# The first k tile for eight column groups, the second for two: another start of a fused decoder layer

## The chip, the cores and the metric

The kernel runs on one core of one Trainium2 chip. The time is device microseconds of one execution; the number given is the median of three runs. The profile shows one execution, whose own time stands beside it. Engines are named as in the profile: PE (TensorE, matmuls), PEld (its weight loads), DVE (VectorE), ACT (ScalarE), POOL, and SP, whose queue issues nearly all DMAs.

## The reference

One decoder layer on 256 tokens with a width of 2048, in float32. What matters here is its beginning:

```python
mod = silu(c) @ w_ada + b_ada            # (6*2048): shift1, scale1, gate1, shift2, scale2, gate2
h   = rms_norm(x, g1) * (1 + scale1) + shift1
p   = h @ w_in                           # 2048 x 12288, columns split into q, k, v, gates of two mixers
# retention and HGRN2 on p, gated, projected, merged, added to x
# then RMSNorm, modulation, w_up, causal conv of width 3, silu(a) * b, w_down, final RMSNorm
```

So the columns of scale1 and shift1 for 128 channels (a k tile) are needed before these channels of h can enter the product with w_in.

## The kernel before

**Tiles.** h has 16 k tiles of 128 channels. The stage around the change multiplies h with the 6144 columns of w_in that the two mixers need, as 12 groups of 512 columns (`ATT`): groups 0 and 1 are the forget gates of HGRN2, 2 and 3 its q, 4 and 5 its inputs, 6 to 11 q, k and v of retention. A piece is one k tile of one group (256 KB of weights). Groups 4, 5, 10 and 11 come out with tokens on the partitions (`mm_rows`, six matmuls of 512 columns for a piece: L187, L188, L189), the others with channels there (`mm_cols`, twelve matmuls of 256 columns: L200, L201, L202). Each product is made of three: high x high, high x low, low x high parts. ACT copies the loaded weights (`raw`) into their high part `wh` (L165), DVE subtracts to get the rest `wl` (L170). L200, L201, L187 and L189 need `wh` only, L202 and L188 need `wl`. There are 12 buffers of `raw`, 4 of `wh` and 4 of `wl`, each for up to two pieces.

**Modulation.** For each k tile, DVE makes four dots of silu(c) with rows of w_ada (L389, 1024 or 1025 columns and 512 KB each; `ada1` loads). ACT turns them into the scale (L400, L401) and the shift (L403) of that tile, and makes the high part of `hT` (L336) and the full value `h` (L340); DVE makes the low part (L341). DVE has multiplied x with the token's norm before (`times`, L379).

**Accumulators.** Groups 0 and 1 are RESIDENT: they stay in four PSUM tiles (`po`) over all 16 k tiles. All other groups share two PSUM tiles of 1024 columns (`pg`): a visit multiplies some k tiles, then `take` moves the sum to SBUF, the first time by an ACT copy (L700, `p<-pg`), later by a DVE addition (L702).

**Order.** The loop at L747 visits the groups in turn. `have` says up to which k tile a visit at the count `work` goes: one k tile more for each ADA_EVERY = 11 pieces. Ahead of the loop stands a part of its own (L705 to L744): the first FIRST = 4 groups take k tiles 0 and 1, both in PSUM, and then groups 2 and 3 are taken. Instructions that pass through `pin` while `self.ordered` is set keep the order in which they are written on their engine; the others (matmuls and `take` among them) are put in place by the scheduler when the program is built. On the chip each engine then runs its list from first to last.

After this stage come the gates' columns, the rest of the mixers, w_out, w_up and w_down.

Of the kernel before, what the change touches and what calls it, by code (L numbers as in the profile page):

```python
# [16 lines left out]
AF = mybir.ActivationFunctionType  # L17
# [12 lines left out]
G = 512  # L30
NORM_EPS = 1e-6
HEAD_EPS = 1e-5
FIRST = 4
RESIDENT = 2
ADA_EVERY = 11
LAG = 1
NOSYNC = mybir.DependencyInfo(mybir.DependencyClass.NoSync, mybir.DependencyReason.DATA)
SMALL = 70

# [16 lines left out]
class Kernel:  # L56
# [609 lines left out]
    def run(self):  # L666
        nc, a = self.nc, self.a
# [11 lines left out]
        def act(k):  # L679
            return hT[k // 2][:, k % 2, :]  # L680

        def ada1(k):
            if k > 0 and k % 2 == 0:
                ins = self.times(k, 2, rx_sb)
                self.tc.add_manual_dep(ins.ins, self.last.ins.name, NOSYNC, reason="behind the weights traced ahead of it")
            yield from self.scale_shift("ada1", k, s1, t1, self.gn1)
            if k % 2 == 0:
                hT[k // 2] = self.blk([P, 2, 2 * T], F32R, name="hT")
            self.modulated(act(k), self.xT[k // 4][:, k % 4, :], k, s1, t1)
            yield 0.7  # L690

        accs = [self.blk([P, NT, G] if c0 in ROWS else [P, 4, T], name="p") for c0 in ATT]
        done = [0] * len(ATT)
        mms = [self.mm_rows if c0 in ROWS else self.mm_cols for c0 in ATT]

        def take(g, ps, fresh):
            for at, z in self.parts(ps, ATT[g] in ROWS):
                dst = accs[g][:, at, :]
                if fresh:
                    nc.scalar.activation(dst, z, AF.Copy)  # L700
                else:
                    nc.vector.tensor_tensor(dst, dst, z, ALU.add)  # L702


        ada = [ada1(k) for k in range(KT)]  # L705
        for _ in range(3):
            next(ada[0])
        rx = self.token_rstd(parts)
        rx_sb = c.tile([P, T], F32, name="rx_sb")
        ps = [self.po2(), self.po2(), self.pg(), self.pg()][:FIRST]  # L710
        for k in range(2):
            for i in range(4 if k else 1):
                if k and i == 1:
                    self.times(k, 1, rx)
                next(ada[k])
            if k == 0:
                self.times(k, 1, rx)

            ahead = 2 * k
            uppers = [self.upper(a["wa"][g][:, k : k + 1, :], 1, G) for g in range(ahead + 1)]  # L720
            rests = [self.rest(z) for z in uppers[:ahead]]
            for _ in ada[k]:
                pass
            for g in range(FIRST):
                if g >= ahead:
                    rests.append(self.rest(uppers[g] if g < len(uppers) else self.upper(a["wa"][g][:, k : k + 1, :], 1, G)))
                wh, wl = rests[g]
                if k == g == 0:
                    self.pin(nc.scalar.activation(rx_sb, rx, AF.Copy))
                mms[g](ps[g], act(k), wh[:, 0, :], wl[:, 0, :], k == 0, k == 1 and g >= RESIDENT)  # L730
        for _ in range(2):
            next(ada[2])
        self.ordered = False
        for gen in ada[2:]:
            self.start(gen, 1)
        for g in range(FIRST):
            done[g] = 2
            if g >= RESIDENT:
                take(g, ps[g], True)
        self.pace(1, 4, ADA_EVERY / 2)  # L740
        self.pace(0, 3.5, 24)

        work = 2 * FIRST
        g = FIRST  # L744
        att, gates = [], []
        small = False
        while min(done) < KT:  # L747
            if work > SMALL and not small:
# [3 lines left out]
                self.start(self.lower_bound())  # L752
            have = min(KT, 2 + int((work - LAG) / ADA_EVERY))
            m = have - done[g]
# [18 lines left out]
            g = (g + 1) % len(ATT)  # L773
            if have == KT and done[0] < KT:
                g = min(i for i in range(len(ATT)) if done[i] < KT)
# [9 lines left out]
        for j in range(4):  # L785
            ps = self.rows(a["wb"][j], act)
# [55 lines left out]
        for j in range(4):  # L842
            last = j == 3
            x1.append(self.load_rows(j))
            g = self.row(self.gate["gate1"], j, "g1")
            ps = self.products(self.mm_rows, self.po2() if last else self.pg(), a["wout"][j], actm, 0, KT, hold=4 * last)
# [14 lines left out]
            if j == 2:  # L861
                part = self.row_part(ss)
# [232 lines left out]
```

## Time and profile before

| | |
|---|---|
| median of 3 runs | 1531.68 us (1531.55 to 1531.72) |
| profiled execution, its own time | 1532.02 us |
| its span | 1529.9 us |
| PE busy | 1511.9 us, 99% |
| DVE busy | 1178.0 us, 77% |
| ACT busy | 841.5 us, 55% |
| DMA | 385.68 MB, mean 252 GB/s |
| granted clock of PE | 0.998 |

The page's first part gives busy time by engine, its fourth the chain of work that ended last, followed back from the end. In a row of a group or of the timeline stand line, engine, operation, output and inputs, shapes and count; behind them, in groups, busy time and mean ns, then idle time ahead of them and what ended it; in the timeline, start and duration in us stand ahead, and a bracket gives the idle time ahead and what ended it. A start-to-start distance is often shorter than the duration, since the next instruction on an engine begins while the last one drains.

### The profile page before, as it was taken

What the parts mean: (1) busy time and instruction counts of PE and PEld (TensorE: products, weight loads), DVE (VectorE), ACT (ScalarE), POOL (GpSimd) and SP (SyncE); (2) the same over time, 40 slices, a digit from 0 to 9 for tenths busy, and PEclk for the clock granted to TensorE, in tenths of its full rate; (3) what the DMA queues carried; (4) which work ended last, traced back from release to release, by engine and by line L of the source; (5) the groups of instructions that cost most, each with busy time, mean ns of one, the idle gap of its engine ahead of it and who ended that gap; (6) DMA issues with size and microseconds to landing.
All of it is one profiled execution on the core that took longest, in us unless ns stands there. A gap on an engine that the chain in (4) does not pass through costs nothing.

```text
span 1529.9 us, 22149 instructions
## 1 busy us (share of the span) xinstructions
PE 1511.9 (99%) x8258; PEld 1304.4 (85%) x8258; DVE 1178.0 (77%) x1610; ACT 841.5 (55%) x1194; POOL 4.0 (0%) x8
## 2 busy tenths in 40 slices
PE   8999999999999999999999999999999999999997
PEld 6999999888888888888878888888888888888886
DVE  7899996997998977898767777777777769455454
ACT  6655455766865554445456565555556558344343
POOL 0000000000000000000000000000000000000000
PEclk9999999999999999999999999999999999999999
DMA  9999996777777789989947777777777766676651
GB/s 375 370 355 328 311 332 217 240 278 239 274 240 264 256 293 323 323 300 341 336 126 231 231 235 233 237 227 232 232 231 232 227 191 192 204 209 206 194 166 55
DMA packets 110992, 385.68 MB, mean 252 GB/s; under 512 B 12802, under 2 KB 13346, under 8 KB 110884
## 3 DMA queue, kind: packets, MB, share of 16 engines
q1 hardware_dynamic: 110016, 383.14, 76.1%
q8 instruction: 64, 1.05, 0.3%
q10 hardware_dynamic: 868, 1.13, 0.2%
q14 instruction: 44, 0.36, 0.1%
HBM read 382.11 MB, written 2.11 MB: 251 GB/s over the span
## 4 chain that ended last, share of the span: by engine, by line
PE 95%; ACT 2%; DVE 1%; DMA 1%; issue 0%; SPq 0%; DVEq 0%; ACTq 0%
PE pg L187 13%; PE pg L188 13%; PE pg L189 13%; PE po L935 11%; PE pg L935 10%; PE po L937 5%; PE pg L937 5%; PE po L189 3%; PE po L187 3%; PE po L188 3%; PE pg L202 3%; PE pg L200 3%; PE pg L201 3%; PE po L565 1%; PE po L200 1%; PE po L201 1%
## 5 line engine op out<-in xcount | busy, mean ns | idle before, releaser
L170 DVE TENSOR_TENSOR wl<-raw,wh 128x1024 fp32r<-128x1024 f32 (+1 forms) x536 | 635.2, 1190 | 286.6 <-ACT wh L165 282.4
L165 ACT ACTIVATE wh<-raw 128x1024 fp32r<-128x1024 f32 (+1 forms) x536 | 551.1, 1033 | 544.1 <-PE pg L189 189.0
L389 DVE SCALAR_TENSOR_TENSOR raw<-raw,sc 128x1024 f32<-128x1024 f32 x192 | 233.5, 1219 | 0.0
L935 PE MATMUL pg<-h2T,wh 128*128 128x512 f32 x704 | 221.6, 396 | 0.6 <-ACT h L371 0.6
L935 PE MATMUL po<-h2T,wh 128*128 128x512 f32 x704 | 221.1, 395 | 0.0
L187 PE MATMUL pg<-wh,hT 128*128 128x512 f32 x512 | 202.7, 396 | 0.2 <-ACT p L700 0.2
L188 PE MATMUL pg<-wl,hT 128*128 128x512 f32 x512 | 200.1, 391 | 0.7 <-DVE wl L170 0.7
L189 PE MATMUL pg<-wh,hT 128*128 128x512 f32 x512 | 199.8, 390 | 0.0
L937 PEld LDWEIGHTS pg<-h2T,wl 128*128 128x128 f32 x704 | 132.1, 188 | 31.7 <-DVE wl L170 0.5
L937 PEld LDWEIGHTS po<-h2T,wl 128*128 128x128 f32 x704 | 132.2, 188 | 31.3
L937 PE MATMUL pg<-h2T,wl 128*128 128x256 f32 x704 | 138.5, 278 | 0.1
L937 PE MATMUL po<-h2T,wl 128*128 128x256 f32 x704 | 138.3, 278 | 0.0
L188 PEld LDWEIGHTS pg<-wl,hT 128*128 128x128 f32 x512 | 96.3, 188 | 21.0 <-DVE wl L170 2.2
L189 PEld LDWEIGHTS pg<-wh,hT 128*128 128x128 f32 x512 | 96.1, 188 | 20.3
L187 PEld LDWEIGHTS pg<-wh,hT 128*128 128x128 f32 x512 | 96.2, 188 | 19.4 <-ACT p L700 0.4
L202 PE MATMUL pg<-hT,wl 128*128 128x256 f32 x384 | 109.1, 284 | 0.6 <-DVE wl L170 0.6
L200 PE MATMUL pg<-hT,wh 128*128 128x256 f32 x384 | 109.2, 284 | 0.1
L201 PE MATMUL pg<-hT,wh 128*128 128x256 f32 x384 | 109.0, 284 | 0.0
L935 PEld LDWEIGHTS pg<-h2T,wh 128*128 128x128 f32 x704 | 107.2, 189 | 0.8 <-ACT h L371 0.8
L935 PEld LDWEIGHTS po<-h2T,wh 128*128 128x128 f32 x704 | 107.2, 189 | 0.0
L202 PEld LDWEIGHTS pg<-hT,wl 128*128 128x128 f32 x384 | 74.1, 193 | 0.8 <-DVE wl L170 0.8
L200 PEld LDWEIGHTS pg<-hT,wh 128*128 128x128 f32 x384 | 74.2, 193 | 0.6 <-ACT wh L165 0.2
(229 smaller groups left out, 2192.0 us busy)
## 6 DMA issues: line engine op xcount, KB each, us to landing
raw<-in_wup SPq DMA_DIRECT2D x176, 512.0 KB, 4.5
raw<-in_wdown SPq DMA_DIRECT2D x88, 512.0 KB, 4.3
raw<-in_wa SPq DMA_DIRECT2D x80, 512.0 KB, 5.7
raw<-in_ada SPq DMA_DIRECT2D x64, 512.5 KB, 5.7
raw<-in_ada SPq DMA_DIRECT2D x64, 512.0 KB, 5.8
raw<-in_wab SPq DMA_DIRECT2D x64, 512.0 KB, 5.0
raw<-in_gate SPq DMA_DIRECT2D x32, 512.5 KB, 4.7
raw<-in_wb SPq DMA_DIRECT2D x32, 512.0 KB, 5.2
```

The lines of the kernel that those rows point to most:

```text
L165: self.pin(self.nc.scalar.activation(wh, raw, AF.Copy))
L170: self.last = self.nc.vector.tensor_tensor(wl, raw, wh.bitcast(F32), ALU.subtract)
L187: nc.tensor.matmul(ps[t], lhsT=hi, rhs=wh, start=first, stop=False)
L188: nc.tensor.matmul(ps[t], lhsT=hi, rhs=wl, start=False, stop=False)
L189: nc.tensor.matmul(ps[t], lhsT=lo, rhs=wh, start=False, stop=last)
L200: nc.tensor.matmul(out, lhsT=wh[:, cs], rhs=hi, start=opens, stop=False, skip_group_check=True)
L201: nc.tensor.matmul(out, lhsT=wh[:, cs], rhs=lo, start=False, stop=False, skip_group_check=True)
L202: nc.tensor.matmul(out, lhsT=wl[:, cs], rhs=hi, start=False, stop=last, skip_group_check=True)
L389: dot = self.pin(nc.vector.scalar_tensor_tensor(raw[:, 0, :], raw[:, 0, :], 1.0, self.sc[:, u * GW : u * GW + w], ALU.mult, ALU.mult, accu ...
L565: nc.tensor.matmul(ps[:, j * 64 : (j + 1) * 64], lhsT=(kt if n > 1 else k)[:, h, c * P : (c + 1) * P], rhs=eq[:, j * 64 : (j + 1) * 64], s ...
L935: self.pin(nc.tensor.matmul(ps[j + z], lhsT=wh[:, cs[z]], rhs=act, start=kt == 0, stop=False))
L937: nc.tensor.matmul(ps[j + z][:, :T], lhsT=wl[:, cs[z]], rhs=act[:, :T], start=False, stop=kt == KT - 1)
```

## The change

The first k tile now runs for eight groups, and the second only for groups 0 and 1, which stay in PSUM. FIRST becomes 8; groups 2 to 7 each get a `pg` tile, one k tile and a `take` at once. The dots of the second k tile are written between groups 3 to 6. `work` starts at 10 in place of 8 and LAG is 7 in place of 1, so the loop begins with group 8 and two k tiles, and the visits after it are of other sizes.

```diff
-FIRST = 4
+FIRST = 8
 RESIDENT = 2
 ADA_EVERY = 11
-LAG = 1
+LAG = 7
...
-        ps = [self.po2(), self.po2(), self.pg(), self.pg()][:FIRST]
-        for k in range(2):
-            for i in range(4 if k else 1):
-                if k and i == 1:
-                    self.times(k, 1, rx)
-                next(ada[k])
-            if k == 0:
-                self.times(k, 1, rx)
-
-            ahead = 2 * k
-            uppers = [self.upper(a["wa"][g][:, k : k + 1, :], 1, G) for g in range(ahead + 1)]
-            rests = [self.rest(z) for z in uppers[:ahead]]
-            for _ in ada[k]:
-                pass
-            for g in range(FIRST):
-                if g >= ahead:
-                    rests.append(self.rest(uppers[g] if g < len(uppers) else self.upper(a["wa"][g][:, k : k + 1, :], 1, G)))
-                wh, wl = rests[g]
-                if k == g == 0:
-                    self.pin(nc.scalar.activation(rx_sb, rx, AF.Copy))
-                mms[g](ps[g], act(k), wh[:, 0, :], wl[:, 0, :], k == 0, k == 1 and g >= RESIDENT)
+        ps = [self.po2(), self.po2()]
+
+        def one(g, k):
+            return self.upper(a["wa"][g][:, k : k + 1, :], 1, G)
+
+        next(ada[0])
+        self.times(0, 1, rx)
+        part = one(0, 0)
+        for _ in ada[0]:
+            pass
+        for g in range(FIRST):
+            wh, wl = self.rest(one(g, 0) if g else part)
+            if g == 0:
+                self.pin(nc.scalar.activation(rx_sb, rx, AF.Copy))
+            to = ps[g] if g < RESIDENT else self.pg()
+            mms[g](to, act(0), wh[:, 0, :], wl[:, 0, :], True, g >= RESIDENT)
+            if g >= RESIDENT:
+                take(g, to, True)
+            done[g] = 1
+            if g >= FIRST - 5 and g < FIRST - 1:
+                next(ada[1])
+            if g == FIRST - 5:
+                self.times(1, 1, rx)
+
+        rests = [self.rest(one(g, 1)) for g in range(RESIDENT)]
+        for _ in ada[1]:
+            pass
+        for g in range(RESIDENT):
+            wh, wl = rests[g]
+            mms[g](ps[g], act(1), wh[:, 0, :], wl[:, 0, :], False, False)
+            done[g] = 2
         for _ in range(2):
             next(ada[2])
         self.ordered = False
         for gen in ada[2:]:
             self.start(gen, 1)
-        for g in range(FIRST):
-            done[g] = 2
-            if g >= RESIDENT:
-                take(g, ps[g], True)
...
-        work = 2 * FIRST
+        work = FIRST + RESIDENT
```

How the built programs differ is seen on ACT first. Before, from the second group's `wh` of the first k tile on (`pg_174` and `pg_175` are groups 2 and 3 in PSUM, `dot` and `s` belong to the second k tile):

```order
L165 ACTIVATE wh_207<-raw_205 128x512
L165 ACTIVATE wh_225<-raw_223 128x512
L165 ACTIVATE wh_243<-raw_241 128x512
L400 ACTIVATE s_125<-dot_259 128x1
L401 ACTIVATE s_125<-gn_85,s_125 128x1
L165 ACTIVATE wh_278<-raw_276 128x512
L165 ACTIVATE wh_283<-raw_281 128x512
L165 ACTIVATE wh_288<-raw_286 128x512
L403 ACTIVATE t_126<-dot_269 128x1
```

Now, from the same place (`pg_227`, `pg_247`, `pg_272`, `pg_289`, `pg_309`, `pg_332` are groups 2 to 7):

```order
L165 ACTIVATE wh_205<-raw_203 128x512
L165 ACTIVATE wh_223<-raw_221 128x512
L700 ACTIVATE p_131<-pg_227 128x1024
L165 ACTIVATE wh_243<-raw_241 128x512
L700 ACTIVATE p_132<-pg_247 128x1024
L165 ACTIVATE wh_268<-raw_266 128x512
L700 ACTIVATE p_133<-pg_272 128x1024
L165 ACTIVATE wh_285<-raw_283 128x512
L700 ACTIVATE p_134<-pg_289 128x1024
L400 ACTIVATE s_125<-dot_261 128x1
L401 ACTIVATE s_125<-gn_85,s_125 128x1
L165 ACTIVATE wh_305<-raw_303 128x512
```

From group 2 on the copy of a group stands between that group's `wh` and the next one's. ACT goes on, at the end of the first k tile (`pg_332` is group 7, `wh_348` and `wh_354` are groups 0 and 1 of the second k tile, `wh_398` is group 8):

```order
L700 ACTIVATE p_136<-pg_332 128x1024
L165 ACTIVATE wh_348<-raw_346 128x512
L165 ACTIVATE wh_354<-raw_352 128x512
L403 ACTIVATE t_126<-dot_299 128x1
L165 ACTIVATE wh_398<-raw_396 128x1024
L336 ACTIVATE hT_184<-xT_95,t_126,s_125 128x256
L340 ACTIVATE h_359<-xT_95,t_126,s_125 128x256
```

The high part of the second k tile's `hT` (L336) now comes behind the copy of group 7 and three `wh`.

On DVE, in the loop, some twenty instructions after its start. Before (`pg_820`, `pg_873` and `pg_929` are sums of groups 2, 3 and 4):

```order
L702 TENSOR_TENSOR p_131<-p_131,pg_820 128x1024
L170 TENSOR_TENSOR wl_933<-raw_930,wh_932 128x1024
L170 TENSOR_TENSOR wl_951<-raw_948,wh_950 128x512
L389 SCALAR_TENSOR_TENSOR raw_960,dot_924<-raw_960,sc 128x1025
L702 TENSOR_TENSOR p_132<-p_132,pg_873 128x1024
L170 TENSOR_TENSOR wl_973<-raw_970,wh_972 128x1024
L341 TENSOR_TENSOR hT_763<-h_965,hT_763 128x256
L170 TENSOR_TENSOR wl_991<-raw_988,wh_990 128x1024
L379 TENSOR_TENSOR xT_96<-xT_96,rx_sb 128x512
L702 TENSOR_TENSOR p_133<-p_133,pg_929 128x1024
```

Now, from the same group's first addition (`pg_554`, `pg_589`, `pg_621` and `pg_647` are sums of groups 2 to 5):

```order
L702 TENSOR_TENSOR p_131<-p_131,pg_554 128x1024
L389 SCALAR_TENSOR_TENSOR raw_666,dot_642<-raw_666,sc 128x1025
L702 TENSOR_TENSOR p_132<-p_132,pg_589 128x1024
L170 TENSOR_TENSOR wl_674<-raw_671,wh_673 128x1024
L341 TENSOR_TENSOR hT_508<-h_703,hT_508 128x256
L702 TENSOR_TENSOR p_133<-p_133,pg_621 128x1024
L170 TENSOR_TENSOR wl_711<-raw_708,wh_710 128x1024
L379 TENSOR_TENSOR xT_96<-xT_96,rx_sb 128x512
L702 TENSOR_TENSOR p_134<-p_134,pg_647 128x1024
L389 SCALAR_TENSOR_TENSOR raw_740,dot_739<-raw_740,sc 128x1024
```

Between two additions there stand now one or two other instructions, where there were three or four. Over the whole stage, the loop's rule makes 70 visits in place of 53, and 54 additions in place of 37.

## The prediction

> **What bounds the kernel now.** I read the page first, then who TensorE waits for, then the stage that the change touches.
>
> ```profile
> span 1529.9 us, 22149 instructions
> PE 1511.9 (99%) x8258; PEld 1304.4 (85%) x8258; DVE 1178.0 (77%) x1610; ACT 841.5 (55%) x1194; POOL 4.0 (0%) x8
> PE 95%; ACT 2%; DVE 1%; DMA 1%; issue 0%; SPq 0%; DVEq 0%; ACTq 0%
> ```
>
> TensorE (PE) holds 95% of the chain that ended last. The change neither adds nor removes a matmul, so it can move the end only by holes in PE's work. The next fence has two answers for that: the windows (columns: stretch and length, then busy time and count of PE, PEld, DVE, ACT, POOL, then granted clock, DMA share, GB/s), and PE's instructions in order of time from its first product to where it no longer waits.
>
> ```profile
> 16.00:40.00 24.00, 21.73 (x129) 19.96 (x130) 20.78 (x35) 15.53 (x27) 0.00 (x0) 1.00 1.03 407
> 95.00:203.00 108.00, 108.00 (x778) 102.44 (x778) 103.13 (x140) 57.78 (x82) 1.91 (x2) 1.00 0.95 334
> ...
> 16.82 0.79 PE L200 MATMUL po<-hT,wh 128*128 128x256 f32 x2 [1.19 <-ACT hT L336]
> ...
> 21.30 0.41 PE L202 MATMUL pg<-hT,wl 128*128 128x256 f32 x1
> 21.51 0.41 PE L200 MATMUL pg<-hT,wh 128*128 128x256 f32 x1
> ...
> 23.01 0.28 PE L202 MATMUL pg<-hT,wl 128*128 128x256 f32 x1
> 23.13 0.28 PE L200 MATMUL pg<-hT,wh 128*128 128x256 f32 x1
> ...
> 33.87 0.39 PE L189 MATMUL pg<-wh,hT 128*128 128x512 f32 x1
> ...
> 35.23 0.39 PE L189 MATMUL pg<-wh,hT 128*128 128x512 f32 x1
> ...
> 39.12 0.39 PE L202 MATMUL pg<-hT,wl 128*128 128x256 f32 x1 [0.55 <-DVE wl L170]
> ```
>
> A 256-column matmul starts every 0.21 us at first (21.30 to 21.51) and every 0.12 us later (23.01 to 23.13). A 512-column one takes 0.227 us (six between 33.87 and 35.23). By the order of PE, 98 of the first kind and 24 of the second stand between 16.82 and 39.12: 98 x 0.12 + 24 x 0.227 = 17.2 us of work in 22.3 us, so 5.1 us are lost there. From 39.12 on PE starts back to back; in 95 to 203 us it is busy 108.00 of 108. The early stretch is fed at 407 GB/s with the DMA share at 1.03, so data arrive no faster. All that a better start can give is those 5.1 us; what a worse one costs is open.
>
> **The change, part by part: the first k tile.** Products, loads and dots keep their prices. New on the way to the end: six of the eight groups are copied out of PSUM after one k tile, and ScalarE (ACT) does that copy where it also makes the high parts (wh) of the weights. In the changed order the copy of a group stands directly ahead of the next group's wh, from the third group on. The copy waits until PE has finished its group, so the next wh cannot start while PE works. The kernel before has this queueing once, at another place, and the trace prices it:
>
> ```profile
> 16.94 1.66 ACT L165 ACTIVATE wh<-raw 128x512 fp32r<-128x512 f32 x3
> 22.29 0.29 ACT L400 ACTIVATE s<-dot 128x1 f32<-128x1 f32 x1 [3.69 <-DVE raw L389]
> 22.62 0.39 ACT L401 ACTIVATE s<-gn,s 128x1 f32<-128x1 f32 x1
> 22.91 1.24 ACT L165 ACTIVATE wh<-raw 128x512 fp32r<-128x512 f32 x2
> 24.40 0.63 ACT L165 ACTIVATE wh<-raw 128x512 fp32r<-128x512 f32 x1 [0.26 <-PE po L201]
> 35.66 1.03 ACT L700 ACTIVATE p<-pg 128x1024 f32<-128x1024 f32 x1 [1.24 <-PE pg L189]
> 36.58 0.28 ACT L403 ACTIVATE t<-dot 128x1 f32<-128x1 f32 x1
> 36.76 1.05 ACT L165 ACTIVATE wh<-raw 128x1024 fp32r<-128x1024 f32 x1
> 37.84 1.83 DVE L170 TENSOR_TENSOR wl<-raw,wh 128x1024 fp32r<-128x1024 f32 x2 [1.94 <-ACT wh L165]
> L170 DVE TENSOR_TENSOR wl<-raw,wh 128x512 fp32r<-128x512 f32 x22 | 15.1, 686 | 5.1 <-ACT wh L165 4.9
> L170 DVE TENSOR_TENSOR wl<-raw,wh 128x1024 fp32r<-128x1024 f32 x73 | 88.6, 1220 | 17.0 <-ACT wh L165 15.3 <-DMA raw<-in_wa 1.7
> ```
>
> The matmul of 35.23 ends at 35.62; the copy starts 0.04 us later, the next ACT instruction 0.92 after the copy's start, wh ends at 37.81, the remainder (wl) starts 0.03 later and PE's L202 starts 0.04 after wl's end. For a piece of 512 columns (wh 0.63, wl 0.69) the way from a group's end to the next group's first use of wl is 0.04 + 0.92 + 0.63 + 0.03 + 0.69 + 0.04 = 2.35 us. The rest of a group of columns is nine more starts and the last matmul: 9 x 0.12 + 0.28 = 1.36, together 3.71. A group of rows: 4 x 0.227 + 0.39 = 1.30, together 3.65. PE needs 1.44 and 1.36 us of work for them.
>
> The third group stands in the same place on every engine as before, so it ends at 23.01 + 0.28 = 23.29. From there: fourth group 27.00, fifth and sixth (rows) 30.65 and 34.30, seventh 34.30 + 3.71 + 0.62 for L400 and L401 ahead of its wh (22.29 to 22.91) = 38.63, eighth 42.34. The six matmuls of the second group that PE has after the fourth lie in its wait. The dots stand between the remainders on DVE and fit into DVE's waits (1.15 us of every 3.7).
>
> Next come the second k tile's activations. They stand on ACT behind the eighth copy, two wh of 512 (0.53 each by the x3 row), L403 (0.18 to the next start) and a wh of 1024 for the ninth group, whose wl PE also needs first: 0.04 + 0.92 + 0.53 + 0.53 + 0.18 + 1.05 + 0.03 + 1.22 + 0.04 = 4.54 us. PE is dense from 42.34 + 4.54 = 46.88. By then it has started 78 matmuls of 256 and 12 of 512: 12.1 us of work. Before, 17.2 us were done at 39.12. The delay is (46.88 - 12.1) - (39.12 - 17.2) = **12.9 us**, and a PE that was busy without a hole afterwards cannot win it back. Bounds: the five chains could be up to 2 us shorter in sum if some wh slipped through; if PE fell to its early pitch they would be longer (a rival below).
>
> Right after, the ninth group's companion piece waits: DVE has hT, times, three dots and wl in front (46.76 + 0.34 + 0.60 + 3 x 1.15 + 1.22 = 52.37 against PE's arrival at 46.88 + 44 x 0.12 = 52.16): 0.2 us.
>
> **The change: smaller visits.** With the new counters a later visit of a group takes two or three k tiles where it took three or four: the visits outside PSUM then need 54 adds (L702) into SBUF in place of 37. Per instruction DVE moves on after 1.14 us, as here:
>
> ```profile
> 101.66 1.22 DVE L702 TENSOR_TENSOR p<-p,pg 128x1024 f32<-128x1024 f32 x1
> 102.79 1.22 DVE L389 SCALAR_TENSOR_TENSOR raw<-raw,sc 128x1024 f32<-128x1024 f32 x1
> ...
> 103.93 1.22 DVE L170 TENSOR_TENSOR wl<-raw,wh 128x1024 fp32r<-128x1024 f32 x1
> L341 DVE TENSOR_TENSOR hT<-h,hT 128x256 fp32r<-128x256 f32 x14 | 5.9, 418 | 0.8 <-ACT h L340 0.8
> L379 DVE TENSOR_TENSOR xT<-xT,rx_sb 128x512 f32<-128x512 f32 x6 | 4.1, 683 | 0.0
> L449 DVE SCALAR_TENSOR_TENSOR ang<-n,ang 128x256 f32<-128x256 f32 x3 | 1.2, 416 | 0.0
> L443 DVE TENSOR_SCALAR ang<-ang,freq 128x256 f32<-128x256 f32 x1 | 0.4, 353 | 0.0
> ```
>
> (The other kinds likewise: the mean less the 0.08 by which the next one starts early.) 17 more adds are 19.4 us. Before, DVE was busy 103.13 of 108.00 us in 95 to 203, so its slack was 4.9 us, 5%, and PE still never waited. In the changed order I take the stretch from the seventh group's visit at work 28 to the first group's at work 102: 74 pieces of one k tile and 512 columns. PE needs 74 x 1.415 (two thirds columns at 1.44, one third rows at 1.36) = 104.7 us. DVE has 27 adds, 26 dots, 30 wl of 1024 (83 x 1.14 = 94.6), 14 wl of 512 and 4 times at 0.60 (10.8), 7 hT at 0.34 (2.4) and the angles (three of L449 and five like L443: 2.8): 110.6 us. DVE needs 5.9 us more than PE, and each excess beyond its lead is a wait of PE. Its lead at the start of the stretch I put at about 2.5 us (ACT gets a wh buffer only when PE has emptied one, two to three pieces ahead). So 3.4 us, and some 0.8 us more because an add that waits for its group now has an hT or a wl behind it: **4.2 us**. Bounds: 0 if the lead is 5.9 us or more; 10.8 if there is none and DVE also keeps its 4.9 us of waits. I stay below the middle since the kernel before ran at 95% without a loss. The later stages keep their instructions, and their slack of DVE is larger.
>
> **Sum.** 12.9 + 0.2 + 4.2 = 17.3 us on the profiled execution's 1532.02 (span 1529.9 and 2.1 around it), which lies 0.3 above the median of 1531.68. Forecast: **1549 us**, 1.1% slower.
>
> **Rivals.** *The clock falls back.* With holes of 1.6 to 2 us in every 3.7, PE could run the starved groups at the early pitch. Priced by the rows: 0.09 us more on each of nine starts and 0.13 on the last for the three groups of columns (3 x 0.97), about 0.9 for each of two groups of rows by the same ratio, and after 46.88 again some 5 us at 0.21 (21.51 is inside such a stretch, which began at 16.82 and had ended by 23.01), or 2.3 us lost: 7.0 in all, **1556 us**. Against it stands the one later place with such holes:
>
> ```profile
> 783.58 1.58 PE L348 MATMUL po<-diag,xr 128*128 128x128 f32 x12 [0.44 <-PE po L189]
> 786.46 1.60 PE L348 MATMUL po<-diag,xr 128*128 128x128 f32 x12 [1.30 <-DVE diag L860]
> 788.71 0.70 PE L935 MATMUL pg<-h2T,wh 128*128 128x512 f32 x2 [0.64 <-ACT h L371]
> ...
> 789.48 0.63 PE L935 MATMUL pg<-h2T,wh 128*128 128x512 f32 x2
> ...
> 790.17 0.63 PE L935 MATMUL pg<-h2T,wh 128*128 128x512 f32 x2
> ```
>
> There PE is idle for most of 5 us, and two matmuls of 512 and two of 256 still take 0.69 us (789.48 to 790.17), the fast pitch. But that lasts 5 us, not 23. [...]
>
> *The adds are free.* DVE's lead covers the excess, and only the start is late: 12.9 + 0.2, **1545 us**. For it: the full lead before. Against: 110.6 over 104.7.
>
> *Faster.* If wh of the fourth to eighth group were made ahead of the copies, PE would have 11.4 us of k = 0 work to cover the second k tile's dots, the waits of the 5.1 us would go and the slow pitch (some 2.4 us) would stay: **1529 us**. It decides at one place, whether ACT starts the fourth wh before 23.29. The order of ACT speaks against it.
>
> *Nothing.* Gains and losses of the start cancel: **1532 us**; it needs the chain of 2.35 us to be hidden, and nothing is queued on PE to hide it but six matmuls.
>
> **How the numbers follow.** Forecast 0.56, clock 0.21, adds free 0.15, faster 0.05, nothing 0.03. The range of 1542 (12.9 less 2, no adds) to 1560 (the clock's case with dearer adds) leaves out the last two and the far tail. Beyond 0.2%, about what a measurement of this kernel can tell from no change, faster gets 0.05, the same 0.03, slower 0.92.
>
> **What would show it.** In the changed profile ACT's L700 should wait for PE six times between 23 and 43 us, with PE's waits for wh and wl behind it, and PE dense only from about 47 us; DVE should be over 97% busy between 75 and 180 us, with PE waits for wl or hT of 2 to 6 us there. A pitch of 0.21 after 25 us would prove the clock's case. I am wrong if the copies don't hold up the next wh, or if PE is dense before 42 us.

## The result, and the profile after

The changed kernel takes 1557.05 us (median, 1555.2 to 1557.4) against 1531.66 of the kernel before in the same session: 1.0162 times as long, with a 95% interval of 1.0148 to 1.0177. Its profiled execution took 1557.27 us. The head of its page:

```profile
span 1555.5 us, 22205 instructions
PE 1522.9 (98%) x8258; PEld 1310.7 (84%) x8258; DVE 1197.2 (77%) x1633; ACT 846.5 (54%) x1201; POOL 4.0 (0%) x8
PE 91%; DVE 4%; ACT 2%; DMA 2%; issue 1%; ACTq 0%; DVEq 0%; SPq 0%
```

PE has the same 8258 matmuls, and its share of the chain fell from 95% to 91%. So the 25.6 us that the span has grown by are holes in PE's work, and matmuls that run slower.

To see where they are I sum, over PE's instructions in order of time, the distance from one start to the next, less the work that stands there: 0.12 us for 256 columns, 0.2275 for 512, and 0.06 to 0.07 set for narrower ones. (That last figure no run shows: 128 columns start 0.11 us apart in both kernels. They are the same matmuls, so it falls out of a difference.) What is left is time lost; such sums agree with the spans to about half a us. Against the kernel before, the changed one loses 17.3 us more up to 75 us (its start), 3.8 us more from 75 to 250 (the loop), and 4.5 us more from 250 to 625 (a late stage); after that nothing. 17.3 + 3.8 + 4.5 = 25.6. The experiments below are split in the same way.

**The start.** First the windows of the kernel before, then those of the changed one (columns as in the prediction).

```profile
20.00:30.00 10.00, 9.32 (x66) 8.91 (x65) 9.38 (x18) 5.31 (x10) 0.00 (x0) 1.00 1.03 404
30.00:40.00 10.00, 9.24 (x53) 7.87 (x53) 7.70 (x11) 7.79 (x12) 0.00 (x0) 1.00 1.03 404
40.00:60.00 20.00, 20.00 (x154) 19.35 (x154) 15.37 (x22) 14.86 (x21) 0.00 (x0) 1.00 1.03 409
75.00:180.00 105.00, 105.00 (x751) 99.30 (x750) 100.54 (x135) 55.95 (x82) 1.91 (x2) 1.00 0.96 338
```

```profile
20.00:30.00 10.00, 7.67 (x38) 6.87 (x36) 2.57 (x5) 3.08 (x4) 0.00 (x0) 0.83 0.96 358
30.00:40.00 10.00, 5.46 (x23) 3.69 (x23) 5.11 (x9) 3.65 (x6) 0.00 (x0) 0.96 0.66 224
40.00:60.00 20.00, 15.09 (x91) 14.15 (x91) 13.30 (x19) 12.35 (x20) 0.00 (x0) 0.68 0.72 224
75.00:180.00 105.00, 103.53 (x720) 96.20 (x719) 104.66 (x135) 52.43 (x78) 0.95 (x1) 1.00 0.90 298
```

Between 20 and 60 us all three engines are now less busy than before, so none of them is short of time: they wait for one another in turn. The granted clock, 1.00 in the rows of before, falls to 0.83, 0.96 and 0.68. (For the first matmuls it says nothing: its rows also read 1.00 ahead of 22.77 us before and of 22.00 now, where matmuls of 256 columns still start 0.21 us apart in both.) PE's waits over the whole execution, grouped (total, times, longest):

```profile
PE pg L200 <- ACT wh L165: 8.8, 4, 3.3
PE pg L187 <- ACT wh L165: 4.3, 3, 2.2
...
PE pg L202 <- DVE wl L170: 2.2, 6, 0.6
```

Between 20 and 60 us nearly all of it is waiting for ACT's high parts (all 8.8 us of the first row and 2.1 of the second), and ACT's timeline says why they are late:

```profile
23.16 1.02 ACT L700 ACTIVATE p<-pg 128x1024 f32<-128x1024 f32 x1 [4.81 <-PE pg L202]
24.09 0.62 ACT L165 ACTIVATE wh<-raw 128x512 fp32r<-128x512 f32 x1
28.03 1.02 ACT L700 ACTIVATE p<-pg 128x1024 f32<-128x1024 f32 x1 [3.32 <-PE pg L202]
...
31.80 1.02 ACT L700 ACTIVATE p<-pg 128x1024 f32<-128x1024 f32 x1 [2.23 <-PE pg L189]
...
35.60 1.02 ACT L700 ACTIVATE p<-pg 128x1024 f32<-128x1024 f32 x1 [2.26 <-PE pg L189]
...
40.60 1.02 ACT L700 ACTIVATE p<-pg 128x1024 f32<-128x1024 f32 x1 [2.86 <-PE pg L202]
...
45.46 1.02 ACT L700 ACTIVATE p<-pg 128x1024 f32<-128x1024 f32 x1 [3.32 <-PE pg L202]
```

Six copies wait for PE, and the weights that PE wants next stand behind each. PE's own timeline, in the first hole and behind the last:

```profile
24.76 0.39 PE L200 MATMUL pg<-hT,wh 128*128 128x256 f32 x1 [1.63 <-ACT wh L165]
...
25.49 0.58 PE L202 MATMUL pg<-hT,wl 128*128 128x256 f32 x1 [0.23 <-DVE wl L170]
25.86 0.42 PE L200 MATMUL pg<-hT,wh 128*128 128x256 f32 x1
26.08 0.41 PE L201 MATMUL pg<-hT,wh 128*128 128x256 f32 x1
...
48.70 0.58 PE L200 MATMUL pg<-hT,wh 128*128 128x256 f32 x1 [3.28 <-ACT wh L165]
...
52.77 0.29 PE L202 MATMUL po<-hT,wl 128*128 128x256 f32 x1
52.89 0.28 PE L201 MATMUL po<-hT,wh 128*128 128x256 f32 x1
```

Behind the hole of 1.63 us the starts are 0.21 to 0.22 us apart (25.86 to 26.08) until 28.6; so they are again from 39.1 to 45.4 and from 48.7 to 52.6, where the distance goes back to 0.12.

**The loop.** From 75 to 180 us DVE is busy 104.66 of 105 us, and PE now waits for it, behind 115.81, 148.32 and at some smaller places. The first of these (PE's timeline):

```profile
116.58 0.39 PE L202 MATMUL pg<-hT,wl 128*128 128x256 f32 x1 [0.48 <-DVE wl L170]
```

**The late stage.** Here nothing of the change stands in the code. Before, PE's wait near 385 us was this (PE's timeline of the kernel before; 0.39 us are missing between the starts of 385.01 and 385.63):

```profile
385.01 0.39 PE L187 MATMUL pg<-wh,hT 128*128 128x512 f32 x1
385.63 0.50 PE L188 MATMUL pg<-wl,hT 128*128 128x512 f32 x1 [0.23 <-DVE wl L170]
```

Now, at the same place of the program (PE's timeline, then ACT's of the changed kernel):

```profile
400.52 0.39 PE L189 MATMUL pg<-wh,hT 128*128 128x512 f32 x1
403.07 0.50 PE L187 MATMUL pg<-wh,hT 128*128 128x512 f32 x1 [2.16 <-ACT wh L165]
404.33 0.80 PE L188 MATMUL pg<-wl,hT 128*128 128x512 f32 x1 [0.76 <-DVE wl L170]
...
406.20 0.63 PE L189 MATMUL pg<-wh,hT 128*128 128x512 f32 x1
406.63 0.63 PE L187 MATMUL pg<-wh,hT 128*128 128x512 f32 x1
```

```profile
387.42 1.06 ACT L165 ACTIVATE wh<-raw 128x1024 fp32r<-128x1024 f32 x1 [3.50 <-PE pg L189]
388.39 0.26 ACT L590 ACTIVATE sqh<-po 128x128 f32<-128x128 f32 x1
...
400.93 1.14 ACT L495 ACTIVATE k<-f,ones 128x1024 f32<-128x1024 f32 x1
401.97 1.04 ACT L165 ACTIVATE wh<-raw 128x1024 fp32r<-128x1024 f32 x1
```

From 388.39 to 401.97 ACT makes no high part; it does the mixers' squares, the second gate's functions and four table loads of 1.28 us. PE uses up what lies ready, waits 2.16 and 0.76 us, and then starts a matmul of 512 columns only every 0.43 us (406.20 to 406.63) until 407.5. From the end of the one `wh` to the start of the next lie 13.5 us of ACT's other work. Before, the longest such block of this stage was 9.2 us (from 374.06 to 383.27). The expectations below speak of 11.6 and 9.0 us; those are estimates from the built orders, and the trace decides.

### The profile page after: what moved, and what is told of

The parts are those of the page before. It is cut to its first block, busy times and chain, and to the rows that moved or that the text cites. A ratio compares the mean times of both kernels' runs of the same rounds, so it can differ in the third digit from the quotient of the medians.

```text
span 1555.5 us, 22205 instructions
## 1 busy us (share of the span) xinstructions
PE 1522.9 (98%) x8258; PEld 1310.7 (84%) x8258; DVE 1197.2 (77%) x1633; ACT 846.5 (54%) x1201; POOL 4.0 (0%) x8
## 3 DMA queue, kind: packets, MB, share of 16 engines
q10 hardware_dynamic: 868, 1.13, 0.2%
## 4 chain that ended last, share of the span: by engine, by line
PE 91%; DVE 4%; ACT 2%; DMA 2%; issue 1%; ACTq 0%; DVEq 0%; SPq 0%
PE pg L188 13%; PE pg L187 13%; PE pg L189 13%; PE po L941 11%; PE pg L941 10%; PE po L943 5%; PE pg L943 5%; PE po L187 3%; PE po L188 3%; PE po L189 3%; PE pg L202 3%; PE pg L200 2%; PE pg L201 2%; DVE wl L170 2%; PE po L565 1%; DVE raw L389 1%
```

## The experiments

The expectations are quoted as they stood before the runs. Times in one line are medians; "start", "loop" and "late" are losses against the kernel before, as above. Runs 1, 3, 4 and 6 were measured beside runs of the kernel before at 1532.29 us, runs 2, 5, 9 and the first of 10 beside 1531.71, run 7 and the last two of 10 beside 1532.44, and run 8 beside 1531.70.

**1. Is it the copy ahead of the next weights?** In the first loop each group's `wh` and `wl` are written one group earlier, and the copies are held in their written order.

```diff
+        uppers = [part]
         for g in range(FIRST):
-            wh, wl = self.rest(one(g, 0) if g else part)
+            while len(uppers) < min(FIRST, g + 1 + 1):
+                uppers.append(one(len(uppers), 0))
+            wh, wl = self.rest(uppers[g])
...
-                    nc.scalar.activation(dst, z, AF.Copy)
+                    self.pin(nc.scalar.activation(dst, z, AF.Copy))
```

> The changed kernel, but the high part of each group's weights is written one group earlier, and the copies out of PSUM keep the written order, so that the next group's wh stands ahead of a group's copy on ACT. By my account (of the 25.4 us, 17.3 are lost before 54 us: 12.9 in the chain copy - wh - wl and 4.4 by the slow pitch in its holes; 3.4 by additions on DVE between 100 and 175 us; 4.6 at one wait near 400 us) the first part goes nearly whole: 1540 to 1542 us, PE dense by about 33 us. Rival: the second k tile comes late because its dots are interleaved with the groups; then the holes move but stay, and the time is above 1552 us.

Measured: 1546.11 us, 1.0089 [1.0074, 1.0104]. Start +4.8, loop +4.1, late +5.6. 12.5 us of the 17.3 at the start are gone by an order alone, so the copy ahead of the weights is the cause. I expected 4 to 6 us more of it. What the start still loses lies mostly in one hole (PE's timeline, then ACT's, of this run):

```profile
36.50 1.22 PE L200 MATMUL po<-hT,wh 128*128 128x256 f32 x4 [2.97 <-ACT hT L336]
```

```profile
33.57 1.02 ACT L700 ACTIVATE p<-pg 128x1024 f32<-128x1024 f32 x1 [1.35 <-PE pg L202]
34.49 1.14 ACT L165 ACTIVATE wh<-raw 128x512 fp32r<-128x512 f32 x2
...
35.85 0.60 ACT L336 ACTIVATE hT<-xT,t,s 128x256 fp32r<-128x256 f32 x1
```

The copy of the eighth group waits for its product, and the whole second k tile (its weights, its shift, its `hT`) stands behind it.

**2. The same for that last copy.** As 1, with the copy of the eighth group behind the second k tile's operands.

```diff
-            if g >= RESIDENT:
+            if g >= RESIDENT and g < FIRST - 1:
                 take(g, to, True)
...
         for _ in ada[1]:
             pass
+        take(FIRST - 1, to, True)
```

> The version with each group's cast one group ahead, and in addition the PSUM copy of the eighth group written behind ACT's conversion of the weights and of the activations for the second k tile. My theory (ACT takes its queue in order, and the one hole of 2.97 us that the start still has is that copy waiting for its product ahead of the next operands): the hole shrinks to about 0.5 us, the start loses 2.3 us against the kernel before in place of 4.8, and the time is 1543.6 us (1543.0 to 1544.4). Rival (the hole is the serial work for the second k tile's activations, their rows and their scale, and the copy is beside it): 1545.8 to 1546.4, as without the edit.

Measured: 1543.72 us, 1.0074 [1.0060, 1.0088]. The hole is 0.58 us now:

```profile
33.07 0.74 PE L200 MATMUL po<-hT,wh 128*128 128x256 f32 x4 [0.58 <-ACT hT L336]
```

Start +2.8, loop +4.5, late +4.6. The time was as expected to 0.1 us. ACT's order, with what the holes do to the clock, makes 14.5 of the 17.3 us.

**3. What the clock adds.** Dummy matmuls of 256 columns (their output is overwritten) fill PE's holes; ACT's order stays as in the changed kernel.

```diff
             to = ps[g] if g < RESIDENT else self.pg()
+            if g > RESIDENT:
+                fill(to[0], 9)
...
+        fill(self.pg()[0], 18)
         rests = [self.rest(one(g, 1)) for g in range(RESIDENT)]
```

> The changed kernel with matmuls that compute nothing of use in PE's holes: 9 to 18 products of 256 columns per hole, from the fourth group on, into PSUM tiles that are written anew behind them; the copies and wh are untouched, so the chain is as long. If PE's pitch falls because PE idles in the holes, it now stays at 0.12 us and the time falls by 4.4 us to about 1552.7 us. Rival: the pitch follows something else; then the time stays at 1557 or rises by the fillers' own time, 1 to 4 us.

Measured: 1554.73 us, 1.0146 [1.0131, 1.0161]. PE's timeline at the first hole (L716 are the dummies):

```profile
23.78 1.30 PE L716 MATMUL pg<-hT 128*128 128x256 f32 x7
24.91 0.28 PE L200 MATMUL pg<-hT,wh 128*128 128x256 f32 x1
...
25.63 0.28 PE L202 MATMUL pg<-hT,wl 128*128 128x256 f32 x1
25.75 0.28 PE L200 MATMUL pg<-hT,wh 128*128 128x256 f32 x1
```

The distance stays 0.12 us where it was 0.21. Start +13.8 (the dummies counted as lost time), loop +3.7, late +4.5: with the clock up, the start costs what the prediction's chain gave, 13.1. In this pair of executions the clock is 3.5 us of the 17.3; how much it is depends on the execution (run 6). The whole time fell by 2.3 us between the medians, and 3.5 between the two profiled spans (1552.0 against 1555.5); with intervals of 2.3 us either way, the size of the term is better read from the matmul starts than from the medians.

**4. The additions, in the kernel before.** The kernel before with LAG = 8 in place of 1: its start as it was, 74 visits and 54 additions.

> The kernel before with LAG = 8: its own start, but visits as small as in the changed kernel (74, with 54 additions on DVE in place of 37). My account: the start is as before, the loop loses 3.4 us (2 to 5), and the late ACT list has the same 11.6 us block between two wh as the changed kernel, so another 4.6 us near 380 us: 1531.7 + 8.0 = 1539.7 us. Rival: with PE's normal start DVE's lead hides the additions, and the late wait belongs to the delayed start: 1532 to 1533 us.

Measured: 1544.25 us, 1.0079 [1.0062, 1.0095]. Start +1.1 (a wait for `wh` of 1.07 us at 64 us, when the small visits have begun), loop +5.8, late +5.0. So small visits alone cost time, with no late start before them. But only 6.9 of the 12 us lie there: most of the late 5.0 us stand at 387 us, with the same waits of 2.16 and 0.76 us as in the changed kernel, and ACT has the same block of 13.5 us there. My account had that block, at 4.6 us, and still came out 4 us too low: the loop cost 5.8 us and not 3.4, outside its bounds of 2 to 5, and the start was not as before.

**5. The additions, in the changed kernel.** LAG = 1 in place of 7: 54 visits and 40 additions, where the changed kernel has 70 and 54.

> The changed kernel with the lag between a group's first and second visit set back from 7 to 1: 54 visits of two k tiles and 40 adds of DVE in place of 65 and 54, the first eight groups as changed. My theory (the 3.8 us that the loop loses are PE's waits for DVE, which has 14 more adds to do): the loop from 75 to 250 us loses 0.5 us or less against the kernel before, the start is as in the changed kernel, and the time is 1553.5 us (1552.8 to 1554.3). Rival (the loop loses them because the late start leaves ACT or DVE behind, whatever the number of adds): 1556.5 us or more.

Measured: 1554.66 us, 1.0143 [1.0130, 1.0157]. One row of the windows:

```profile
75.00:180.00 105.00, 105.00 (x725) 98.20 (x725) 102.45 (x141) 56.56 (x82) 0.95 (x1) 1.00 0.96 325
```

DVE has 2.55 us of slack again in these 105, and PE none: loop +0.1 in place of +3.8. That settles the loop. The time came out 1.2 us above what I expected, and outside the range, since a new wait of 1.28 us for a copy came at 56 us (start +18.5), and late is +4.8.

**6. The late block.** One background task is told to last 123 us in place of 122; the scheduler then spreads ACT's late work otherwise, and its largest block there is 6.9 us long in the trace (6.7 by the built order).

```diff
-        self.pace(0, 122.0, 88)
+        self.pace(0, 123.0, 88)
```

> The changed kernel with one pacing constant of a later stage at 123 in place of 122. The first 300 us keep their instructions; on ACT the block of mixer work that stands between two wh near 400 us shrinks from about 11.6 us to 6.7 us of instructions. My account: the wait of 2.2 us plus 0.8 us there and the slow pitch behind it go, 1557.05 - 4.6 = 1552.5 us. Rival: that wait is a late effect of the delayed start (a backlog on ACT or DVE); then it stays and the time stays within 1 us of 1557.

Measured: 1553.98 us, 1.0143 [1.0128, 1.0158]. Start +15.8, loop +3.8, late +3.0. The waits of 2.16 and 0.76 us are replaced by 0.66, 0.26 and 0.94 at three places, at the full clock (512 columns 0.23 us apart behind each). A part of the late loss goes with the block, less than I expected, and 3.0 us stay, spread over smaller waits. So neither expectation holds whole. The start has the instructions of the changed kernel and still lost 1.5 us less: here the clock first fell at 38.5 us, there at 25.4. From copy to copy ACT's rows of this run give 3.81, 3.79, 3.78, 4.56 and 4.86 us.

**7. The late block, in the kernel before.** The same line with 124.0, which there makes the block 12.3 us in the trace where it was 9.2 (10.9 and 9.0 by the built orders), and changes nothing of the start.

> The kernel before with only the duration of one background task changed, 124 in place of 122, so that the scheduler puts 10.9 us of ACT's late instructions between two conversions of weights, where it put 9.0 us (11.6 us in the changed kernel). Nothing of the first 300 us changes. My theory (the changed kernel lost about 4.5 us near 400 us to the place of such a block alone): the wait for the weights near 385 us, 0.39 us so far, grows by 1.9 us and the time with it, to 1533.5 us, or to 1535 if the clock falls in that hole too (1533.0 to 1535.5). Rival (the late loss comes from the state in which the changed loop leaves the buffers, and not from the block): 1531.3 to 1532.2.

Measured: 1534.27 us, 1.0012 [1.0003, 1.0021]. PE's timeline:

```profile
384.05 0.49 PE L187 MATMUL pg<-wh,hT 128*128 128x512 f32 x1 [0.98 <-ACT wh L165]
385.31 0.50 PE L188 MATMUL pg<-wl,hT 128*128 128x512 f32 x1 [0.76 <-DVE wl L170]
385.65 0.40 PE L189 MATMUL pg<-wh,hT 128*128 128x512 f32 x1
```

The kernel before gets the changed kernel's waits by the place of ACT's work alone, smaller by the smaller block, and the clock holds (512 columns 0.23 us apart from 385.65 on). The block is 1.2 us shorter than the changed kernel's, and the two waits together are 1.2 us shorter (1.74 against 2.92). The medians are 1.8 us apart, as expected (0.5 to 3.2 by the interval); in the profiled execution late is +1.6, and the start, where the instructions are the same, +0.8. There the distance between starts goes from 0.21 to 0.12 us at 19.70 and not at 22.77, PE then lost 1.0 us more in its next wait, near 24, and from 26.85 to 29.83 the starts were 0.21 us apart again. So the account of one execution can be 1 us off by the clock alone. Whether each of the changed kernel's 4.5 us has this cause is not shown; that a block of this kind makes the wait near 400 us, which with the slow matmuls behind it is 4.6 us, is.

**8. The dots in between.** The changed kernel with the second k tile's dots behind the eight groups.

```diff
-            if g >= FIRST - 5 and g < FIRST - 1:
-                next(ada[1])
-            if g == FIRST - 5:
-                self.times(1, 1, rx)
+        for i in range(4):
+            next(ada[1])
+            if i == 0:
+                self.times(1, 1, rx)
```

> The changed kernel with one part of the change undone: the four dots of the second k tile stand behind the eight groups, as they stood behind the four groups in the kernel before, and not in between. My theory (the chain of copy, high part, remainder and products sets the start, DVE waits 1.9 to 2.7 us for ACT at every group, and the dots in between only fill that): without them the remainder of the eighth group ends at about 42.2 us, since L400 and L401 no longer stand ahead of the seventh group's cast (0.6 us), four dots and the products with rx take 4.9 us from there, and the activations of the second k tile come at about 48 us, as they do now: 1557.0 us (1556.0 to 1558.0). Rival (the dots in between take 4 x 1.15 us off the path, as they are meant to): 1560 us or more.

Measured: 1557.65 us (1555.27 to 1560.47), 1.0171 [1.0152, 1.0191]. The median agrees with "they only fill a wait"; the interval, wide in this run, does not exclude a cost of 3 us. Its four times fall apart, into 1555.3 twice and 1560.0 and 1560.5; the profile is of one of the first two. Start +15.4, loop +3.8, late +4.5. The second k tile's first matmul starts at 47.40 us without the dots in between, and at 49.30 in the changed kernel, but there the clock fell much earlier. The fairer comparison is run 6, with the changed kernel's start and a clock that held until 38.5 us (here 41.2): 47.66. So in these executions the dots bought next to nothing, since ACT paced the groups and DVE waited in any case. What made the two times of 1560 us is not known, and the rival is not excluded for them.

**9. Is the start of the kernel before bound by the clock?** It runs its first 28 matmuls at 0.214 us until 22.77. Dummy matmuls of 128 columns (results unused) in two holes ahead of its first product:

```diff
+        for _ in range(2):
+            nc.tensor.matmul(warm[:, :P], lhsT=parts[-1][:, :P], rhs=self.ones, start=True, stop=True)
         q = self.small([P, NT], name="rq")
...
+        for _ in range(2):
+            nc.tensor.matmul(warm[:, :P], lhsT=q[:, 0:1].to_broadcast([P, P]), rhs=self.ident, start=True, stop=True)
         return ps
```

> The kernel before with four dummy fp32 matmuls of 128 columns (their output is thrown away) in PE's two holes ahead of its first product, between the row sums, the transposed scale and the first weights. The kernel before runs its first 28 matmuls of 256 columns at a pitch of 0.214 us to 22.77 us, then at 0.12. If the clock comes up by how busy PE was in the stretch before, these run at 0.12 and up to 28 x 0.094 = 2.6 us go: 1529.7 us (1529.0 to 1531.0), with the pitch of 0.12 from 17 us on. Rival (the dummies hold up the chain by their own 0.2 to 0.4 us each, or the first product is bound by its weights and not by PE): 1531.7 to 1532.8.

Measured: 1532.34 us, 1.0001 [0.9992, 1.0010]. Both theories missed: the clock did come up, at 18.5 us, and PE was at the end of this work 1.8 us earlier (23.36 in place of 25.16), but the time stayed, where the rival had put it for other reasons. PE's timeline:

```profile
18.43 0.31 PE L202 MATMUL po<-hT,wl 128*128 128x256 f32 x1
18.58 0.27 PE L200 MATMUL po<-hT,wh 128*128 128x256 f32 x1
...
23.36 0.28 PE L202 MATMUL pg<-hT,wl 128*128 128x256 f32 x1
25.77 0.74 PE L200 MATMUL po<-hT,wh 128*128 128x256 f32 x4 [2.13 <-ACT hT L341]
```

It now stands 2.13 us for the second k tile's `hT`, 25.77 where it was 25.91. DVE sets that, with four remainders and four dots back to back (9.38 us busy in 20 to 30 us, above). PE's slow matmuls had lain in its shade. That the dummies alone brought the clock up is not shown: in run 7's execution it came up at 19.70 us without any.

**10. Everything at once, and fewer groups.** First: 2 with LAG = 1, the late line of 6 and the dummies of 9.

> The version with casts one group ahead and the eighth group's copy late, with the lag of 1, the other late pace on ACT and the dummy matmuls ahead of the first product: every cause that I hold for the changed kernel's loss is taken out, while eight groups of the first k tile still come first. If the accounts add up: start +2.3, loop +0.4, late +1.5, warm clock -2.6, against 1531.7, so 1533.3 us (1532.0 to 1535.0). Rival (the terms overlap, since a gap that goes in one place comes back at the next wait): 1537 us or more.

Measured: 1538.17 us, 1.0039 [1.0026, 1.0051]. Start +2.4, loop +1.3, late +2.4, and 0.6 us for the dummies. The accounts did not add up: the 2.6 us for the clock came back at the next wait, as in 9, and the loop and the late part kept 0.9 us more each.

Then, since 9 showed a hole of 2.13 us that PE could fill with other groups of the first k tile: six groups in place of eight, `wh` two groups ahead, the last two copies behind the second k tile's operands, LAG = 1, the late line as before (a block of 9.2 us) and the dummies; and the same with five groups.

> A version that the runs so far point to: the first k tile for six groups (not eight), casts two groups ahead, the copies of the last two of them behind the second k tile's operands, its dots in between, a lag of 1, the dummy matmuls that warm the clock, and the late block of 9.0 us as in the kernel before. In the version of the kernel before with the dummies PE stood 2.13 us at 23.4 us for DVE's dots; here it has two more groups (2.9 us) to do at that time, and DVE has no more to do than before. If that is so: 2.1 us less than the kernel before at the start, up to 0.8 us more for three more adds, 1530.4 us (1529.5 to 1531.3). Rival (the copies or the adds take it back, as in the run with every cause removed): 1531.7 us or more.

> The same with five groups: one more group (1.44 us) for the hole of 2.13 us, and one copy behind the second k tile's operands. By the same account: 1.4 us less at the start, up to 0.8 us more for adds, 1531.0 us (1530.0 to 1531.8). Rival: 1532 us or more.

Measured: 1534.05 us with six, 1.0010 [1.0001, 1.0019], and 1534.34 with five, 1.0012 [1.0004, 1.0021]. No gain in either: with six the start is +0.7, the loop +1.1, late +1.1, and more by the dummies; with five +0.9, +0.5 and +1.1. The condition that they were built on was not met in these executions: with the same dummies the clock came up only at 22.1 us with six groups and 21.5 with five. PE's larger share of work is there, but the second k tile's `hT` is still waited for (0.82 us with six groups, 1.58 with five), and the next tiles' `wl` behind it (1.13 and 1.14). On ACT that `hT` again stands, with two `wh` and the shift, behind a copy that waits for its product (at 25.90 with six groups and 25.05 with five). No kernel that I ran beats the one before.

## Why the prediction was right, and where it was not

**The chain copy, high part, remainder (12.9 us): right in mechanism, and in size at the full clock.** From copy to copy it gave 3.71, 3.65, 3.65, 4.33 and 3.71 us. ACT's rows give 4.87, 3.77, 3.80, 5.00 and 4.86: the groups of rows are right to 0.15 us, the groups of columns 0.7 to 1.2 us longer, and those ran wholly or partly at the slow pitch. In run 6, at the full clock until 38.5 us, the first four are 3.81, 3.79, 3.78 and 4.56, all within 0.25 us. With the clock kept up (3) the start cost 13.8 us against 12.9 + 0.2, and with the order of ACT mended (1 and 2) nearly all of it went.

**The clock was on the wrong side of the chances.** The rival had it at 7.0 us with a chance of 0.21, and the forecast had none of it. The pitch of 0.21 after 25 us, named as its proof, is there. The account of the start exceeds the chain by 4.2 us, and the fillers took off 3.5; in run 6 the same start exceeds it by 2.7. The rival's price was too high, because groups of rows kept the clock (512 columns 0.23 us apart behind 30.68 and 34.46) and one group of columns kept it for half its length (0.12 us apart up to 39.10, 0.21 behind 39.30). The step that failed was to judge by the one place at 783 us, and it was misread. PE is not idle there for most of 5 us: the three rows have holes of 0.44, 1.30 and 0.64 us, 2.4 of 5.1. The longest of them is shorter than the holes of 1.63 and, near 37 us, 2.23 that went ahead of the falls in the changed kernel (last section). That holes of about 2 us keep the clock was the author's assumption: in these runs it held through holes of 1.63 us at some places and fell behind one at another.

**Smaller visits (4.2 us, bounds 0 to 10.8): right.** Measured 3.8 in the changed kernel, gone to 0.1 with LAG = 1, and 5.8 (6.9 with the wait at 64 us) when put into the kernel before. DVE was to be over 97% busy from 75 to 180 us, and was at 99.7%. "The adds are free" is refuted.

**"The later stages keep their instructions, and their slack of DVE is larger" was the step that failed outright.** They keep them, but not their order on ACT: the program is scheduled as a whole, and the other instructions ahead moved ACT's late work into one longer stretch without a `wh` (13.5 us in place of 9.2). The late stage lost 4.5 us, which are in no term and no rival. Run 7 shows that such a block makes the wait; run 6 shows that with the block cut to 6.9 us 3.0 of the loss stay, so for a part of it the cause is open. The difference of the built orders shows the place; the prediction used it for the start and the loop, and not there.

**The sum** came to 17.3; measured by the account, 17.3 (start, for 13.1) + 3.8 (loop, for 4.2) + 4.5 (late, for 0) = 25.6. So 1557.05 lies inside the range, 8 us above the forecast, and about half of the miss is the clock and half the late stage. The range reached so far up for the clock's case with dearer additions. That it also holds the late 4.5 us, which stood in no case, is luck.

**"Faster" (1529 us, with `wh` ahead of the copies)** was a condition that runs 1 and 2 made true, and the start was still 2.8 us slower than before. The step behind that price, that PE's 5.1 us of early loss would go once PE had more work, was wrong for the kernel before: DVE sets that part (run 9). With eight groups, what keeps the last 2.8 us was not separated: in run 2 PE waits in turn for ACT (0.47 us for `wh`, 0.58 for `hT`) and for DVE, longest 1.13 us for a `wl` that stands behind two dots.

## What to carry to other kernels

ACT took its instructions in the order in which they stand (its rows above follow the built order; the copy of 23.16 had waited 4.81 us, and the `wh` behind it starts at 24.09). A copy that waits for a product must not stand ahead of the conversion that feeds the next product (in run 1 that order alone was worth 12.5 us); count, for each engine in between, what is queued behind each instruction that waits. Where a scheduler orders the whole program, compare the built order of every stage, above all the longest stretch on each engine without the instruction that feeds the bound, and not only of the stage that was edited. And a slow engine ahead of a wait is no gain to be had (in run 9 PE was done 1.8 us earlier, and the time stayed): look first at who is late at the next meeting point.

## What was not expected of the hardware

In the changed kernel the clock fell behind holes of PE of 1.63 us (ahead of 24.76) and 2.23 us (ahead of 37.80). The distance between the starts of 256-column matmuls changes near 22.0, 25.5, 28.9, 39.1 and 52.8 us, and with it the granted clock (windows, columns as in the prediction):

```profile
22.04:25.45 3.41, 1.59 (x11) 1.18 (x10) 0.71 (x2) 1.54 (x2) 0.00 (x0) 1.00 1.05 400
25.45:28.87 3.42, 3.38 (x16) 3.39 (x16) 1.46 (x3) 0.84 (x1) 0.00 (x0) 0.50 0.88 301
28.87:39.10 10.23, 5.22 (x20) 3.05 (x20) 5.00 (x8) 4.35 (x8) 0.00 (x0) 1.00 0.68 244
39.10:52.76 13.66, 8.75 (x38) 7.94 (x37) 6.58 (x11) 6.66 (x10) 0.00 (x0) 0.50 0.60 185
```

In the two stretches that end with a fall PE was busy for 1.59 of 3.41 us and for 5.22 of 10.23. The length of one hole does not tell: the stretch from 28.87 to 39.10 held through a hole of 1.63 us too (ahead of 33.39), and in run 6 the starts were still 0.12 us apart from 25.56 on, behind the same hole (1.63 us, ahead of 24.61). What decides when the clock falls is not shown.

Keeping PE busy with dummy work held the clock (3: 0.12 us from start to start behind 25.63), which was worth 3.5 us in the profiled execution. Whether dummies raise it earlier (9) is not settled: with them ahead of the first product the starts went to 0.12 us at 18.58 us in run 9, but only at 22.09 and 21.49 in the last two of 10; without them at 22.77 in the kernel before, and at 19.70 in run 7. In run 9, where it came earlier, the time stayed (1532.34 us).
